# One Trainium2 kernel, diagonal softmax: y of five steps loaded through ScalarE's queue, and all row sums of six steps on VectorE

## The chip, the cores and the metric

The kernel runs on one core of one Trainium2 chip. The metric is the device time of one execution in microseconds; the median of the timed runs counts. The core has a VectorE (DVE in the profile), a ScalarE (ACT), a SyncE (SP) that mainly issues transfers, and 16 DMA engines that move data between HBM and the on-chip memory of 128 partitions. SyncE and ScalarE each have a DMA queue of their own, q1 and q10 in the profile.

## The reference

For each of 8 batches, x and y are 4096 x 512 in float32. Of the product x yT only the diagonal is needed, that is, one dot product of 512 elements per row; a softmax over the 4096 dot products of a batch follows.

```python
def reference(x, y):
    gram = np.matmul(x, y.transpose(0, 2, 1))
    diag = np.diagonal(gram, axis1=1, axis2=2)
    diag = diag - diag.max(axis=-1, keepdims=True)
    exp = np.exp(diag)
    return (exp / exp.sum(axis=-1, keepdims=True)).astype(np.float32)
```

x and y together are 134.2 MB, each byte of which is read once. The output is 0.13 MB.

## The kernel before

Four batches (Q) lie side by side on the 128 partitions, 32 partitions each; a partition holds 128 rows of its batch (C). So the work is two halves of four batches. Each half is cut into four steps of R = 32 rows a partition, which makes S = 8 steps, numbered 0 to 7. A step loads 128 x 32 x 512 elements of x and as many of y, 8.39 MB each.

The on-chip memory has two places for x, `xs[0]` and `xs[1]`, used in turn, and only one for y, `ys`. A small buffer `side` holds K = 6 rows of y.

Steps 0 to 5 are one loop, lines 123 to 134. In step t:

- `load_x` (line 65) and `load_y` (line 68) are issued by SyncE. x(t) may be issued when the sums of step t-2 have freed its place; y(t) when the first 26 rows of products of step t-1 have been made and the other 6 rows of y copied away.
- ScalarE copies the last 6 rows of y into `side` (line 126).
- VectorE multiplies the first 26 rows of x by `ys`, in place (line 72), then the last 6 rows by `side`.
- VectorE sums 30 rows of products (line 75), and ScalarE the last W = 2 rows (line 80).

At the end of step 3 the softmax of the first half begins (`exps`, line 101), and in step 4 it is ended (`normalize`, line 109). Step 6 splits its work otherwise: part of y is copied into a free part of x's other place (line 140), and ScalarE sums 30 of the 32 rows. Step 7 loads x and y in nine pieces, all on SyncE, and makes each row's dot product with one VectorE instruction (line 85). The softmax of the second half and the output follow.

The order of instructions on each engine is the order in which the kernel writes them, and an instruction that waits holds up all that stands behind it on its engine. On SyncE the loads thus stand as x(0), y(0), x(1), y(1), x(2) and so on. In this text x(t) and y(t) are the loads of step t, and "the sums" or "the products" of a step are its instructions of lines 75 and 72.

Of the kernel before, what the change touches and what calls it, by code (L numbers as in the profile page):

```python
# [1 line left out]

# [5 lines left out]


@with_exitstack
def kernel(
    ctx: ExitStack,
    tc: tile.TileContext,
    x: bass.AP,
    y: bass.AP,
    out: bass.AP,
):
    nc = tc.nc
    ctx.enter_context(tc.manual_schedule())  # L20
    f32 = mybir.dt.float32
    Alu = mybir.AluOpType
    Act = mybir.ActivationFunctionType
    X = mybir.AxisListType.X
    B, N, D = x.shape
    P = nc.NUM_PARTITIONS
    G = 32
    Q = P // G
    C = N // G
    R = 32  # L30
    H = R // 2
    K = 6
    W = 2
    F = H + 1
    L = 9
    S = B // Q * (C // R)


    xv = x.rearrange("(s b) (j c) d -> s (b j) c d", b=Q, j=G)
    yv = y.rearrange("(s b) (j c) d -> s (b j) c d", b=Q, j=G)  # L40
    ov = out.rearrange("(s b) (j c) -> s (b j) c", b=Q, j=G)

    big = ctx.enter_context(tc.tile_pool(name="big", bufs=1))
    small = ctx.enter_context(tc.tile_pool(name="small", bufs=1))


    xs = [big.tile([P, R, D], f32, name=f"xs{i}") for i in range(2)]
    ys = big.tile([P, R, D], f32, name="ys")
    side = big.tile([P, K, D], f32, name="side")

    diag = [small.tile([P, C + 2 * i], f32, name=f"diag{i}") for i in range(B // Q)]
    res = [small.tile([P, C], f32, name=f"res{i}") for i in range(B // Q)]

    def columns(t, r0, n):
        c0 = t % (C // R) * R + r0
        return slice(c0, c0 + n)

    def rows(t, r0, n):
        return xs[t % 2][:, r0 : r0 + n, :]

    def dots_of(t, r0, n):
        return diag[t * R // C][:, columns(t, r0, n)]

    def load_x(t, r0, n):
        nc.sync.dma_start(out=rows(t, r0, n), in_=xv[t * R // C, :, columns(t, r0, n), :])  # L65

    def load_y(t, r0, n):
        nc.sync.dma_start(out=ys[:, r0 : r0 + n, :], in_=yv[t * R // C, :, columns(t, r0, n), :])  # L68

    def products(t, r0, n, yt):  # L70
        xt = rows(t, r0, n)
        nc.vector.tensor_tensor(out=xt, in0=xt, in1=yt, op=Alu.mult)  # L72

    def sums(t, r0, n):
        nc.vector.tensor_reduce(out=dots_of(t, r0, n), in_=rows(t, r0, n), axis=X, op=Alu.add)  # L75

    def sums_act(t, r0, n):
        for r in range(r0, r0 + n):
            row = xs[t % 2][:, r, :]
            nc.scalar.activation(out=row, in_=row, func=Act.Copy, accum_out=dots_of(t, r, 1))  # L80

    def dots(t, r0, n):
        for r in range(r0, r0 + n):
            xt = xs[t % 2][:, r, :]
            nc.vector.scalar_tensor_tensor(  # L85
                out=xt, in0=xt, scalar=1.0, in1=ys[:, r, :], op0=Alu.mult, op1=Alu.mult,
                accum_out=dots_of(t, r, 1),
            )

    def over_quadrant(name, column, op, negate=False):  # L90

        got = small.tile([P, 1], f32, name=name)
        nc.vector.tensor_reduce(  # L93
            out=got, in_=column.to_broadcast([P, G]), axis=X, op=op, negate=negate, apply_transpose=True
        )
        return got

    def largest(out, d):
        nc.vector.tensor_reduce(out=out, in_=d, axis=X, op=Alu.max)  # L99

    def exps(i, d):
        mxp = small.tile([P, 1], f32, name=f"mxp{i}")
        largest(mxp, d)
        nmx = over_quadrant(f"nmx{i}", mxp, Alu.max, negate=True)
        sump = small.tile([P, 1], f32, name=f"sump{i}")
        nc.scalar.activation(out=res[i], in_=diag[i][:, :C], func=Act.Exp, bias=nmx, scale=1.0, accum_out=sump)  # L106
        return sump

    def normalize(i, sump):
        total = over_quadrant(f"sum{i}", sump, Alu.add)  # L110
        rc = small.tile([P, 1], f32, name=f"rc{i}")
        nc.vector.reciprocal(out=rc, in_=total)  # L112
        nc.vector.tensor_single_scalar(out=res[i], in_=res[i], scalar=rc, op=Alu.mult)  # L113

    nc.vector.addr_align(128, offset=0, max_nops=0)
    nc.scalar.addr_align(128, offset=0, max_nops=0)

    nc.sync.drain()  # L120
    nc.sync.drain()  # L121

    for t in range(S - 2):
        load_x(t, 0, R)
        load_y(t, 0, R)
        nc.scalar.activation(out=side, in_=ys[:, R - K :, :], func=Act.Copy)  # L126
        if t == C // R:
            normalize(0, sump)
        products(t, 0, R - K, ys[:, : R - K, :])
        products(t, R - K, K, side)  # L130
        sums(t, 0, R - W)
        sums_act(t, R - W, W)
        if t == C // R - 1:
            sump = exps(0, diag[0])

    t = S - 2
    load_x(t, 0, R)
    load_y(t, 0, R)
    spare = rows(t + 1, R - L, L)
    nc.scalar.activation(out=spare, in_=ys[:, F - L : F, :], func=Act.Copy)  # L140
    products(t, 0, F - L, ys[:, : F - L, :])
    products(t, F - L, L, spare)
    products(t, F, R - F, ys[:, F:, :])
    sums(t, R - W, W)
    sums_act(t, 0, R - W)
    largest(diag[1][:, C + 1 :], diag[1][:, : C - 2 * R])


    t += 1
    upto = {load_x: 0, load_y: 0}  # L150
    done = 0
    for load, n in (
        (load_x, H - 1), (load_y, F), (load_x, 8), (load_y, 10), (load_x, 6), (load_y, 3), (load_x, 2), (load_y, 2), (load_x, 1)
    ):
        load(t, upto[load], n)
        upto[load] += n
        both = min(upto.values())
        dots(t, done, both - done)
        done = both
        if done == F:  # L160
            largest(diag[1][:, C : C + 1], diag[1][:, C - 2 * R : C - R + H])

    met = small.tile([P, C - R], f32, name="met")
    nc.scalar.activation(out=met, in_=diag[1][:, : C - R], func=Act.Copy)  # L164

    for p in range(0, P, H):
        nc.sync.dma_start(out=ov[0, p : p + H, :], in_=res[0][p : p + H, :])
    normalize(1, exps(1, diag[1][:, C - R + H :]))
    nc.scalar.dma_start(out=ov[1], in_=res[1])


# [1 line left out]
_INS = ['x', 'y']  # L173
_OUTS = [((8, 4096), 'float32')]


# [23 lines left out]
```

## Time and profile before

| what | value |
|---|---|
| time, median of 3 runs | 320.38 us (320.29 to 320.44) |
| span of the profiled execution, first to last instruction | 318.8 us |
| around the span, median less span | 1.6 us |
| VectorE busy | 241.7 us (76%) |
| ScalarE busy | 49.8 us (16%) |
| 26 products of a step on VectorE | 14.03 us |
| 6 products | 3.35 us |
| 30 sums | 16.15 us |
| one row sum on ScalarE | 0.617 + 0.187 us |
| copy of 6 rows of y on ScalarE | 2.76 us |
| read from HBM | 134.22 MB, 421 GB/s over the span |

The profiled execution has no separate time beside its span; the 1.6 us are taken from the timed runs. In the views, L72 is line 72 of the kernel; `xs<-in_x_dram` is a transfer into `xs`; "SPq" and "ACTq" are the issues of transfers by SyncE and ScalarE; the time in brackets or after "waited for" is idle time of the engine that waits. The view of a window cuts it into 40 equal slices and gives what DMA moved in each, in GB/s; a packet is booked at its start, so a slice can show more than DMA can move.

### The profile page before, as it was taken

The numbers are of one execution on the slowest core, as the hardware profiler recorded it, in microseconds if no ns is written. First come the engines' busy times: TensorE is split into PE (matmuls) and PEld (weight loads), VectorE is DVE, ScalarE is ACT, GpSimd is POOL, SyncE is SP. The second block draws the span as 40 slices with busy tenths as digits, with TensorE's granted clock in tenths as the row PEclk, the third lists the DMA queues.
The fourth block names the chain that finished last, engine by engine and source line by source line (L and its number), as shares of the span: only waits on it lengthen the run. The fifth ranks groups of instructions, "written<-read, shape, count | busy, mean of one in ns | idle before, by whom it ended". The sixth has DMA issues, their size and how long they took to land.

```text
span 318.8 us, 315 instructions
## 1 busy us (share of the span) xinstructions
DVE 241.7 (76%) x98; ACT 49.8 (16%) x97; POOL 0.2 (0%) x4
## 2 busy tenths in 40 slices
DVE  0000069995899939999399994999939998599996
ACT  1000030100301003010120103000030100596700
POOL 0000000000000000000000000000000000000000
DMA  9999999999999999999999999999999999999993
GB/s 372 419 395 469 452 395 452 469 395 395 493 428 395 469 452 395 428 477 411 395 485 436 395 469 452 395 403 493 419 395 469 452 395 452 394 440 410 429 411 112
DMA packets 3714, 134.37 MB, mean 421 GB/s; under 512 B 512, under 2 KB 768, under 8 KB 1280
## 3 DMA queue, kind: packets, MB, share of 16 engines
q1 hardware_dynamic: 3568, 134.29, 97.7%
q10 hardware_dynamic: 144, 0.07, 0.1%
q14 instruction: 2, 0.02, 0.0%
HBM read 134.22 MB, written 0.13 MB: 421 GB/s over the span
## 4 chain that ended last, share of the span: by engine, by line
DMA 65%; DVE 33%; SPq 1%; issue 0%; ACT 0%; DVEq 0%
DMA ys<-in_y_dram 65%; DVE xs L72 32%; DVE xs L85 0%; SPq L65 0%; SPq L68 0%; DVE res L113 0%; DVE sum L93 0%; DVE nmx L93 0%; ACT res L106 0%; DVE mxp L99 0%; DVE rc L112 0%; DVEq L72 0%; SPq L121 0%; SPq L120 0%
## 5 line engine op out<-in xcount | busy, mean ns | idle before, releaser
L72 DVE TENSOR_TENSOR xs<-xs,ys 128x13312 f32<-128x13312 f32 (+2 forms) x8 | 96.7, 12091 | 71.9 <-DMA ys<-in_y_dram 71.9
L75 DVE TENSOR_REDUCE diag<-xs 128x30 f32<-128x15360 f32 (+1 forms) x7 | 98.1, 14020 | 0.2
L80 ACT ACTIVATE xs<-xs 128x512 f32<-128x512 f32 x42 | 25.9, 617 | 90.4 <-DVE xs L72 90.4
L126 ACT ACTIVATE side<-ys 128x3072 f32<-128x3072 f32 x6 | 16.6, 2763 | 124.1 <-DMA ys<-in_y_dram 124.1
L85 DVE SCALAR_TENSOR_TENSOR xs<-xs,ys 128x512 f32<-128x512 f32 x32 | 19.9, 687 | 1.1 <-DMA ys<-in_y_dram 1.0
L72 DVE TENSOR_TENSOR xs<-xs,side 128x3072 f32<-128x3072 f32 x6 | 20.1, 3351 | 0.0
L80 ACT ACTIVATION_READ_ACCUMULATOR xs<-xs 128x1 f32 x42 | 7.9, 187 | 0.0
L140 ACT ACTIVATE xs<-ys 128x4608 f32<-128x4608 f32 x1 | 4.0, 4043 | 20.0 <-DMA ys<-in_y_dram 20.0
L106 ACT ACTIVATE res<-diag,nmx 128x128 f32<-128x128 f32 x2 | 0.8, 402 | 30.1 <-DVE nmx L93 30.1
L72 DVE TENSOR_TENSOR xs<-xs,xs 128x4608 f32<-128x4608 f32 x1 | 5.0, 4951 | 0.0
L85 DVE DVE_READ_ACCUMULATOR xs<-xs,ys 128x1 f32 x32 | 2.6, 82 | 0.0
L126 ACT ACT_TABLE_LOAD x1 | 1.3, 1283 | 1.2 <-PEq L184 1.2
L93 DVE TRANSPOSE_TENSOR_REDUCE sum<-sump 128x1 f32<-128x32 f32 x2 | 0.4, 212 | 1.2 <-ACT res L106 1.2
L113 DVE TENSOR_SCALAR res<-res,rc 128x128 f32<-128x128 f32 x2 | 0.6, 286 | 0.1
L99 DVE TENSOR_REDUCE mxp<-diag 128x1 f32<-128x128 f32 (+1 forms) x2 | 0.5, 229 | 0.1
L93 DVE TRANSPOSE_TENSOR_REDUCE nmx<-mxp 128x1 f32<-128x32 f32 x2 | 0.4, 211 | 0.1
L99 DVE TENSOR_REDUCE diag<-diag 128x1 f32<-128x64 f32 (+1 forms) x2 | 0.4, 202 | 0.0
L112 DVE RECIPROCAL rc<-sum 128x1 f32<-128x1 f32 x2 | 0.3, 164 | 0.1
L106 ACT ACTIVATION_READ_ACCUMULATOR res<-diag,nmx 128x1 f32 x2 | 0.4, 186 | 0.0
L164 ACT ACTIVATE met<-diag 128x96 f32<-128x96 f32 x1 | 0.3, 283 | 0.0
L184 POOL MEMSET const-bfloat16-1.0<- 128x1 bf16 x1 | 0.1, 102 | 0.0
L184 POOL MEMSET const-uint8-127<- 128x1 uint8 x1 | 0.1, 101 | 0.0
(2 smaller groups left out, 0.2 us busy)
## 6 DMA issues: line engine op xcount, KB each, us to landing
ys<-in_y_dram SPq DMA_DIRECT2D x1, 4352.0 KB, 14.9
xs<-in_x_dram SPq DMA_DIRECT2D x1, 3840.0 KB, 14.2
ys<-in_y_dram SPq DMA_DIRECT2D x1, 2560.0 KB, 12.9
xs<-in_x_dram SPq DMA_DIRECT2D x1, 2048.0 KB, 19.4
xs<-in_x_dram SPq DMA_DIRECT2D x1, 1536.0 KB, 16.3
ys<-in_y_dram SPq DMA_DIRECT2D x1, 768.0 KB, 17.7
xs<-in_x_dram SPq DMA_DIRECT2D x1, 512.0 KB, 18.5
ys<-in_y_dram SPq DMA_DIRECT2D x1, 512.0 KB, 19.3
```

The source lines that it names most:

```text
L72: nc.vector.tensor_tensor(out=xt, in0=xt, in1=yt, op=Alu.mult)
L75: nc.vector.tensor_reduce(out=dots_of(t, r0, n), in_=rows(t, r0, n), axis=X, op=Alu.add)
L80: nc.scalar.activation(out=row, in_=row, func=Act.Copy, accum_out=dots_of(t, r, 1))
L85: nc.vector.scalar_tensor_tensor(out=xt, in0=xt, scalar=1.0, in1=ys[:, r, :], op0=Alu.mult, op1=Alu.mult, accum_out=dots_of(t, r, 1),)
L93: nc.vector.tensor_reduce(out=got, in_=column.to_broadcast([P, G]), axis=X, op=op, negate=negate, apply_transpose=True)
L99: nc.vector.tensor_reduce(out=out, in_=d, axis=X, op=Alu.max)
L106: nc.scalar.activation(out=res[i], in_=diag[i][:, :C], func=Act.Exp, bias=nmx, scale=1.0, accum_out=sump)
L112: nc.vector.reciprocal(out=rc, in_=total)
L113: nc.vector.tensor_single_scalar(out=res[i], in_=res[i], scalar=rc, op=Alu.mult)
L126: nc.scalar.activation(out=side, in_=ys[:, R - K :, :], func=Act.Copy)
L140: nc.scalar.activation(out=spare, in_=ys[:, F - L : F, :], func=Act.Copy)
L164: nc.scalar.activation(out=met, in_=diag[1][:, : C - R], func=Act.Copy)
```

## The change

The y loads of steps 1 to 5 are no longer written at the head of their step for SyncE's queue. Each is written one step earlier, behind the 26 products that free its place, and is issued by ScalarE. x stays on SyncE's queue, as do y of step 0 and all loads of steps 6 and 7. The last two row sums of steps 0 to 5 move from ScalarE to VectorE, which then sums all 32 rows with one instruction.

```diff
-    def load_y(t, r0, n):
-        nc.sync.dma_start(out=ys[:, r0 : r0 + n, :], in_=yv[t * R // C, :, columns(t, r0, n), :])
+    def load_y(t, r0, n, queue=nc.sync):
+        queue.dma_start(out=ys[:, r0 : r0 + n, :], in_=yv[t * R // C, :, columns(t, r0, n), :])
...
     for t in range(S - 2):
         load_x(t, 0, R)
-        load_y(t, 0, R)
+        if t == 0:
+            load_y(t, 0, R)
         nc.scalar.activation(out=side, in_=ys[:, R - K :, :], func=Act.Copy)
         if t == C // R:
             normalize(0, sump)
         products(t, 0, R - K, ys[:, : R - K, :])
+        if t < S - 3:
+            load_y(t + 1, 0, R, nc.scalar)
         products(t, R - K, K, side)
-        sums(t, 0, R - W)
-        sums_act(t, R - W, W)
+        sums(t, 0, R)
         if t == C // R - 1:
             sump = exps(0, diag[0])
```

## The prediction

> **What bounds the kernel now.** I read the page's first lines, then the chain of waits, then one step of the timeline, then the DMA view of a few short windows. The page says that VectorE is busy for 76% of the span, yet the queue that carries the loads is full:
>
> ```profile
> span 318.8 us, 315 instructions
> DVE 241.7 (76%) x98; ACT 49.8 (16%) x97; POOL 0.2 (0%) x4
> q1 hardware_dynamic: 3568, 134.29, 97.7%
> HBM read 134.22 MB, written 0.13 MB: 421 GB/s over the span
> ```
>
> Queue q1 (SyncE's) keeps the 16 DMA engines at work for 97.7% of the span. The chain in order of time shows how that looks inside the steps:
>
> ```profile
> 56.62 24.50 DMA ys<-in_y_dram
> ...
> 81.21 14.04 DVE xs L72
> ...
> 95.30 24.52 DMA ys<-in_y_dram
> ...
> 119.91 14.04 DVE xs L72
> ```
>
> The chain alternates "26 products, y load" and repeats every 38.70 us (81.21 to 119.91). It names VectorE for 14 us of each step, but that is not 14 us in which DMA rests. The stretches say so (columns: stretch, length, DVE busy, ACT busy, POOL busy, PE clock, DMA share, GB/s):
>
> ```profile
> 42.51:81.21 38.70, 33.44 (x3) 4.03 (x6) 0.00 (x0) 1.00 1.00 434
> 81.21:119.91 38.70, 33.45 (x3) 4.10 (x6) 0.00 (x0) 1.00 1.00 434
> 119.91:158.61 38.70, 33.45 (x4) 4.11 (x6) 0.00 (x0) 1.00 1.00 434
> 158.61:197.31 38.70, 34.60 (x8) 4.65 (x8) 0.00 (x0) 1.00 1.00 434
> ```
>
> DMA share is 1.00 in every step. A step moves x and y, 2 x 128 x 32 x 512 x 4 B = 16.78 MB; at 434 GB/s that is 38.7 us, the whole period. So the kernel is a stream of loads without a hole. The first step's products start at 42.51; the last piece of the other seven pairs of loads releases VectorE at 313.26, 270.75 us for 7 x 38.7 = 270.9. There is no idle DMA time to win back. The head (about 3 us above two loads) and the tail (318.8 - 313.3 = 5.5 us) are not touched.
>
> **How much cover each load has.** A load is 8.39 MB, 19.35 us. On each of 16 engines it is 8 packets (a 9.7 us window in mid-load has 64 packets for 4.19 MB, so 64 KB each), 2.42 us a packet. A y load takes 24.50 us from issue to landing, so it queues behind x. The smallest load-independent delay is seen at the end: the last output is issued by ScalarE at 316.43, and a window there shows its first packet at 317.30, so 0.87 us. Around 78 us the packets of all engines run in waves (slices of 0.1 us, starting at 76.0):
>
> ```profile
> GB/s 0 0 0 0 0 0 0 0 0 0 0 0 0 1966 1311 1966 655 0 1311 655 655 655 1311 0 0 0 0 0 0 0 0 0 0 0 0 0 0 1311 1966 1966
> ```
>
> A packet is booked where it starts, 655 is one packet. The wave of 77.3 to 78.3 (3, 2, 3, 1, 0, 2, 1, 1, 1, 2: 16 packets) is the last of y(1): it ends 79.7 on the first engine, 80.7 on the last, and VectorE starts at 81.21, about 0.5 us later. From an empty queue a load would thus take 0.87 + 19.35 + 0.5 + some 0.1 = 20.8 us. Spare of a y load: 24.5 - 20.8 = 3.7 us. Spare of an x load: x(2) is issued at 76.06, can start at 76.93, and is needed at 79.7 to 80.7: 2.8 to 3.8 us.
>
> **The change, part by part.**
>
> *y goes to ScalarE's queue.* Before, SyncE waits for exactly the same event, the 26 products:
>
> ```profile
> SPq L68 <- DVE xs L72: 169.3, 8, 53.6
> SPq L65 <- DVE diag L75: 114.4, 6, 19.1
> ```
>
> The x load ahead of it on SyncE is long issued (76.06 against 95.30), so y(2) leaves at 95.30, 0.05 us after the products end at 95.25. On ScalarE it leaves at the same time; an issue lasts 0.38 us there (the output's row) against 0.33 us, and the 0.05 us is under the 3.7 us spare. "As soon as its place is free" already held. Queued behind the waiting issue on ScalarE are the next copy into `side`, which needs that y anyway, and in step 3 the exponential, which runs at 192.82 while its y issue stands at 172.70. Nobody waits. On SyncE, x(t+2) no longer passes the y wait, but its own wait (for the sums) ends 19.4 us later, so it gains nothing. y(0), y(6) and y(7) stay on SyncE.
>
> *ScalarE's two row sums go, VectorE sums 32 rows.* Removed from ScalarE: 2 x (0.617 + 0.187) = 1.6 us a step, in time in which it then idles 20 us. Added to VectorE: 2/30 of 16.15 us = 1.08 us in each of six steps. VectorE idles 5.22 us before each y (3.24 us before step 4, where the softmax of the first half stands), so 4.1 and 2.2 us remain: nothing on the path. But x(t+2) waits for these sums, so it is issued 1.08 us later: x(2) at 77.14, at the engines at 78.01. Its spare falls to 1.7 to 2.7 us. Still no hole. If that cover were gone, each step would pay up to 1.08 us, 6.5 us in all.
>
> *Two queues at once.* This is the only real novelty, and the trace of before shows no load on another queue than q1, so it is bounded from both sides. y(2) reaches the engines at 96.17 and meets the last 2.9 to 3.9 us of x(2); x(3) meets the last packet of y(2). As long as an engine always has a packet, the order does not change when both are through, and the period stays 38.7 us. The Trainium skill speaks against a gain here: in "DMA: Bandwidth & Descriptors", "Issuing engines are not separate DMA queues", it says that loads issued by different engines run on the same 16 DMA engines and interleave. By that rule the sum stays at 0; the 434 GB/s with a share of 1.00 agrees.
>
> Lower end of this cost: an engine's 16 packets of 2.42 us fill the period of 38.70 us to within 0.1 us, the reading's own fineness; 0.1 us in each of seven steps would be -0.7 us. Upper end: the two rivals below, +4.4 and +6 us. I take 0, being nearest to the rows of four steps that stay at 1.00 whatever else happens in them.
>
> Sum: 0 (y issue) + 0 (ScalarE) + 0 (VectorE, hidden) + 0 (queues) + 0.1 (issue times). The profiled execution would keep its 318.8 us of span; the timed runs have 1.6 us around that (320.38). I say 320.5.
>
> **Rivals.**
>
> *A load's end waits its turn: slower.* A load is reported by a small marker packet behind its eight (the window 76 to 80 counts 8 packets under 512 B in the wave of load ends). If an engine takes turns between queues after each packet, an x packet goes ahead of y's marker. x(2) reaches the engines at 78.01; by the wave above, 12 engines are then in y(1)'s last packet and lose one turn (2.42 us), but 4 start it later and lose two (4.84 us); the slowest counts. One turn fits into the spares (3.7 and 2.7 us) and costs nothing. Two turns do not: y(2), issued 4.84 us late, leaves a hole of 4.84 - 3.7 = 1.1 us, and x(3) one of 4.84 - 1.1 - 2.7 = 1.0 us, 2.1 to 2.2 us for a pair of steps. Three pairs bound it at 6.6 us, one at 2.2; two pairs give +4.4: 324.8 us. It decides at 0.25 us: were x there after 78.3, all would be single turns. Against it: an engine that chooses its next packet only slightly ahead has that 0.25 us. The Trainium skill ("DMA: Bandwidth & Descriptors", "Queues, rings and completion order") says that an engine drains a whole packet of about 9 to 17 descriptors from one ring before it switches. Eight pieces and a marker are nine; were they one such packet, turns would fall between loads and this rival would be void; no run here shows which.
>
> *Changing queues costs time: slower.* From rest the first packets take longer: in windows of the first 8 us the waves start at 1.8 and at 4.7, 2.9 us apart instead of 2.42, so some 0.5 us. If every change of queue cost that, five changes a step over five steps are up to 12.5 us; half of it is +6: 326.4. Against: at the ends of loads within q1 the waves stay 2.42 us apart.
>
> *Two queues close small pauses: faster.* At most the 0.7 us above: 319.7. Against: the share is 1.00 already.
>
> **Chances.** No change 0.52 (own range 320.1 to 321.0), marker's turn 0.27, queue changes 0.13, faster 0.08. A measurement of this kernel can tell about 0.2%, 0.64 us, from no change. Both slower rivals are above it: slower 0.40, same 0.52, faster 0.08. The range reaches from 319.9, which leaves out most of the faster case, to 325.0, which takes in the middle of the marker case and leaves out its top and half of the queue changes: under 2 in 10 outside.
>
> **What would show it.** Right: y landings still 38.7 us apart, a DMA share of 1.00 in each stretch, y's issues on ScalarE at 56.6, 95.3 and so on, x's issues 1.08 us later (77.14, 115.83), VectorE idle about 4.1 us before each y, x landing later by a packet or two without effect. Marker's turn: products of step 1 start 2.4 or 4.8 us late while those of step 2 are nearly on time, every second step late, DMA share below 1.00 near 100 and 121 us. Queue changes: share at 1.00 but under 434 GB/s in steps 1 to 5. The forecast is wrong if products of step 6 start later than 275.4 (274.78 + 0.64).

## The result: 7.5 us slower, and the profile after

The changed kernel takes 327.86 us (median of four runs, 327.26 to 328.57) against 320.37 us: 1.0234 times as long, interval 1.0219 to 1.0248. The prediction said 320.5 us, with a range of 319.9 to 325.0. It was wrong; the time lies beyond the range, on the side of the two slower rivals. In the ratios of this text, runs more than 1.5% above the fastest of the same kernel are not counted.

The page's first parts of the changed kernel (columns as before):

```profile
span 326.3 us, 286 instructions
DVE 248.0 (76%) x98; ACT 41.8 (13%) x73; POOL 0.2 (0%) x4
q1 hardware_dynamic: 2848, 92.34, 66.6%
q10 hardware_dynamic: 864, 42.01, 30.2%
HBM read 134.22 MB, written 0.13 MB: 412 GB/s over the span
```

The five y loads, 42 MB, are now on q10. Both queues together hold the DMA engines for 96.8% of 326.3 us, 315.9 us; before it was 97.8% of 318.8 us, 311.8 us (q1 97.7%, q10 0.1%). The bytes are the same. So of the 7.5 us some 4.1 are packets that take longer, and only some 3.4 are time in which engines stand idle. VectorE has 6.3 us more work, close to the 6 x 1.08 that was worked out. The chain in order of time (start, length, what):

```profile
42.27 14.04 DVE xs L72
...
56.39 26.82 DMA ys<-in_y_dram
...
83.30 14.04 DVE xs L72
...
97.41 24.17 DMA ys<-in_y_dram
...
121.68 14.04 DVE xs L72
...
135.79 27.68 DMA ys<-in_y_dram
...
163.57 14.04 DVE xs L72
```

The y loads no longer all take 24.5 us: they take 26.8, 24.2, 27.7, then 22.6, 28.5 and, on SyncE again, 23.2. On a grid of 38.70 us from 42.27, the products of steps 1 to 6 start 2.3, 2.0, 5.2, 3.4, 7.4 and 6.0 us late. Every second step adds lateness, and the next one wins back only a part. Step 7 adds 1.8 us: from the start of step 6's products to that of the last four dot products it takes 40.3 us (280.49 to 320.79) instead of 38.5. The stretches between these starts (length, DVE, ACT, POOL, clock, DMA share, GB/s):

```profile
42.27:83.30 41.03, 34.51 (x3) 2.70 (x2) 0.00 (x0) 1.00 1.00 434
83.30:121.68 38.38, 34.52 (x4) 2.77 (x2) 0.00 (x0) 1.00 0.98 410
121.68:163.57 41.89, 34.51 (x4) 2.76 (x2) 0.00 (x0) 1.00 1.01 435
163.57:200.42 36.85, 35.68 (x9) 3.32 (x4) 0.00 (x0) 1.00 0.99 416
200.42:243.15 42.73, 34.51 (x3) 2.70 (x2) 0.00 (x0) 1.00 0.98 417
243.15:280.49 37.34, 34.52 (x4) 2.75 (x1) 0.00 (x0) 1.00 0.97 407
280.49:320.79 40.30, 37.40 (x67) 22.92 (x62) 0.00 (x0) 1.00 0.96 404
```

The first two long steps are not short of DMA: 434 and 435 GB/s, a share of 1.00. In them DMA moves more than the step needs, because part of the next x goes ahead of the end of y. The loss comes in the steps after, at 410 and 416 GB/s. From the third long step on, every step is below the rate of before, the long one too (417 GB/s). The rate falls further than the share: at 410 GB/s it is 6% down, and the share only 2%, so there too packets take longer.

How x gets ahead is seen at the end of y(1). Two windows of the changed kernel, 79.6 to 80.6 and 82.6 to 83.1 us (queue: packets, MB, share):

```profile
q1 hardware_dynamic: 16, 1.05, 242.9%
q10 hardware_dynamic: 11, 0.00, 0.6%
...
q1 hardware_dynamic: 6, 0.39, 181.5%
q10 hardware_dynamic: 5, 0.00, 0.6%
```

On q10 only markers are left, packets of 4 B that report a load's end. In the first window 11 of 16 engines send theirs. All 16 start their first packet of x(2). The other 5 engines do so ahead of their marker, and these five markers follow only when that packet is through, 2.42 us later. VectorE waits for the last of them. In the kernel before, the window of 79.6 to 80.8 us holds all 16 markers. At the end of y(3) two engines put a packet of x ahead of their marker, and the last of them was late already. At the end of y(5) all 16 do: the window of 238.8 to 240.4 us has 16 packets of q1 and no marker, that of 241.2 to 242.8 us the 16 markers. It is one packet each time.

And how the loss comes after it: y(2), issued at 97.41, in the window of 97.4 to 101.4 us (slices of 0.1 us):

```profile
GB/s 655 0 0 0 0 0 0 0 0 0 0 0 0 0 0 0 0 2622 655 0 1311 655 1311 655 0 655 0 655 655 0 0 0 0 655 655 0 0 0 0 0
q10 hardware_dynamic: 16, 1.05, 70.7%
```

The first value is x(2)'s last packet. x(2) ended from 99.1 on, and y(2)'s first packets start over 1.8 us, from 99.1 to 100.9, the last 3.5 us after the issue. Some engines had nothing to do meanwhile. And q10's share, 70.7% of 4.0 us for one packet on each of 16 engines, makes 2.83 us a packet, where 2.42 is usual. At the end of y(2), with hardly an engine idle, the first packets of x(3) are as long (window of 117.8 to 121.8 us, 2.82 us a packet):

```profile
q1 hardware_dynamic: 16, 1.05, 70.5%
```

### The profile page after: what moved, and what is told of

It is laid out like the page before. It is cut to its first block, busy times and chain, and to the rows that moved or that the text cites. A ratio compares the mean times of both kernels' runs of the same rounds, so it can differ in the third digit from the quotient of the medians.

```text
span 326.3 us, 286 instructions
## 1 busy us (share of the span) xinstructions
DVE 248.0 (76%) x98; ACT 41.8 (13%) x73; POOL 0.2 (0%) x4
## 4 chain that ended last, share of the span: by engine, by line
DMA 66%; DVE 32%; SPq 1%; issue 1%; ACT 0%; DVEq 0%; ACTq 0%
DMA ys<-in_y_dram 66%; DVE xs L72 31%; DVE xs L85 0%; SPq L65 0%; SPq L68 0%; DVE res L113 0%; DVE sum L93 0%; DVE nmx L93 0%; ACT res L106 0%; DVE mxp L99 0%; DVE rc L112 0%; DVEq L72 0%; ACTq L68 0%; SPq L121 0%; SPq L120 0%
## 5 line engine op out<-in xcount | busy, mean ns | idle before, releaser
L75 DVE TENSOR_REDUCE diag<-xs 128x32 f32<-128x16384 f32 (+1 forms) x7 | 104.5, 14934 | 0.2
L80 ACT ACTIVATE xs<-xs 128x512 f32<-128x512 f32 x30 | 18.4, 614 | 2.8 <-DVE xs L72 2.8
L80 ACT ACTIVATION_READ_ACCUMULATOR xs<-xs 128x1 f32 x30 | 5.6, 186 | 0.0
```

## The experiments

Theory M: the end of a y load waits its turn behind an x packet of the other queue, and the loads issued from that late point find engines that are already empty. Rival C: an engine loses time at each change of queue. Rival A: ScalarE's queue itself is slower.

**The sums alone.**

```diff
 # kernel before
-        sums(t, 0, R - W)
-        sums_act(t, R - W, W)
+        sums(t, 0, R)
```

> Only the sums move: VectorE sums all 32 rows in steps 0 to 5, every load stays on SyncE's queue. Theory M (with two queues the end of a y load waits its turn behind an x packet, and the loads that follow then come too late to find the engines busy): no effect, 320.4 us, at most +0.5, because x(t+2) is issued 1.08 us later but still lies behind y on the same queue. Theory C (each change of queue costs an engine a pause): 320.4. Theory A (ScalarE's queue itself is slower): 320.4. If the later x alone were the cause, it would show here as +1.08 us in each of six steps, 326.9.

Measured: 320.71 us against 320.61, ratio 1.0007, interval 0.9995 to 1.002. The y loads take 24.50, 24.74, 24.53, 24.51, 24.52 and 24.56 us. The 1.08 us of VectorE and the later x are hidden while one queue carries the stream.

**The queue alone.**

```diff
 # changed kernel
-        sums(t, 0, R)
+        sums(t, 0, R - W)
+        sums_act(t, R - W, W)
```

> Only the queue moves: y of steps 1 to 5 on ScalarE's queue, ScalarE keeps the two row sums, so x is issued 1.08 us earlier than in the changed kernel. M: more engines have x before the last y packet, so the first late y is 2.4 to 4.8 us late; in all +4 to +9 us, 324 to 329. C and A: as the changed kernel, 327.9.

Measured: 325.68 us (four runs from 324.3 to 329.2), ratio 1.0141, interval 1.0119 to 1.0164. By the ratio the second queue alone costs 4.5 us; the sums, free alone, cost some 3 us more beside it. C and A have no place for that difference. M may have one, as x is issued 1.08 us later after a late y, but no run shows that this is the reason. The first step goes as M said, with its products 2.4 us late; the pattern of every second step does not hold here, for step 2's are 4.3 us late.

**One queue, but ScalarE's.**

```diff
 # changed kernel
         if t == 0:
-            load_y(t, 0, R)
+            load_x(0, 0, R, nc.scalar)
+            load_y(0, 0, R, nc.scalar)
+            load_x(1, 0, R, nc.scalar)
...
         sums(t, 0, R)
+        if t < S - 3:
+            load_x(t + 2, 0, R, nc.scalar)
```

The other issues of x up to step 6 are taken out.

> All x and y loads of steps 0 to 5 and x of step 6 on ScalarE's queue, in the order of the kernel before; VectorE sums 32 rows; y of step 6 and step 7 on SyncE. One queue carries the stream, so no y end meets an x packet of another queue. M: the loss goes, 320.4 plus up to 0.6 for ScalarE's later start. C: goes too, 320.4 to 321. A: stays or grows, 328 or more, as twice the bytes run on that queue.

Measured: 323.09 us, ratio 1.0077, interval 1.0065 to 1.009: 2.5 us, more than the 0.6 allowed and far from A's 8. The timeline and the chain of this run show where:

```profile
1.16 2.55 ACTq L65 DMA_DIRECT2D xs<-in_x_dram  x1
...
44.72 14.04 DVE xs L72
...
83.41 14.04 DVE xs L72
```

ScalarE's first issue lasts 2.55 us, where SyncE's lasts 0.40 us, and y(0) is issued at 3.74 instead of 1.28. From there the steps are 38.7 to 39.1 us. So the head costs 2.45 us and the queue itself next to nothing. A falls.

**Smaller x packets.** Two runs with x in pieces of 8 rows, the second with step 6 too, and the same pieces on one queue as a control.

```diff
-        load_x(t, 0, R)
+        for r in range(0, R, R if t < 2 else R // 4):
+            load_x(t, r, R if t < 2 else R // 4)
...
 # second run and control also
-    load_x(t, 0, R)
+    for r in range(0, R, R // 4):
+        load_x(t, r, R // 4)
```

> The changed kernel with x of steps 2 to 5 loaded in four pieces of 8 rows, so that an x packet is 16 KB and takes 0.6 us instead of 2.4. M: the end of a y load waits 0.6 to 1.2 us instead of 2.4, the products of step 1 start about 82.0 instead of 83.3, and little of the loss is left: 320.5 to 323. C: as many changes of queue or more, 328 or more. A: 327.9.

Measured: 325.17 us, ratio 1.0129, interval 1.0089 to 1.0168: above M's 323, below C's 328, so it decides nothing alone. Its y(1) took 24.98 us, but its y(5), which meets x of step 6, left whole there, 28.53 us. Hence the next two.

> The changed kernel with x of steps 2 to 6 in four pieces (x of step 6 too, which the run with x in quarters left whole, and whose y before it came 5 us late). M: every y end waits 0.6 to 1.2 us only; step 6's products start near 276 instead of 280.5; 321 to 323.5. C or A: 325 or more, as with step 6 whole.

> Control: the kernel before, one queue, with x of steps 2 to 6 loaded in four pieces of 8 rows. M, C and A: 320.4, within 0.5; smaller packets alone cost nothing while one queue holds the order. If pieces themselves cost, 321 to 323.

Measured: 322.70 us for two queues, ratio 1.0078, interval 1.006 to 1.0096; 322.16 us for one queue, ratio 1.0059, interval 1.0044 to 1.0073. The control is not free, though 320.4 us was expected first: four pieces cost 1.8 us. But with small packets the second queue, and the sums with it, add only 0.5 us to that, instead of 7.5. That is within M's 321 to 323.5 and below the 325 of C and A. Step 6's products start at 276.24 us, where M had said 276. The chain with two queues, then with one:

```profile
56.37 25.10 DMA ys<-in_y_dram
...
81.56 14.04 DVE xs L72
...
134.03 25.67 DMA ys<-in_y_dram
```

```profile
56.43 24.49 DMA ys<-in_y_dram
...
81.02 14.03 DVE xs L72
...
133.99 24.80 DMA ys<-in_y_dram
```

y(1) is 0.6 us late and y(3) 0.9, where whole x packets made it 2.3 and 3.2. A turn of 16 KB takes 0.6 us, one of 64 KB 2.42. The delay follows the size of the other queue's packet.

**Smaller y packets.** y of steps 1 to 5 in four pieces on ScalarE's queue, x whole.

> The changed kernel with y of steps 1 to 5 in four pieces of 8 rows on ScalarE's queue, x whole on SyncE's: y's packets take 0.6 us and x's 2.4. M: each of the last two or three y packets and y's last marker waits behind an x packet, 3 to 4 turns of 2.4 us, so the products of step 1 start 5 to 10 us late (86 to 91 us), and each such step loses some 4 to 9 us: 333 to 347. C: one more change of queue for each small packet, at 0.5 us a change 2 us a step, 338 at most, with lateness spread over all steps. A: 327.9.

Measured: four runs from 325.1 to 339.8 us, median 333.5, too wide for a ratio. In the profiled one, the fastest, step 1's products start at 83.50, one turn late and not three or four. ScalarE's four issues of y(1) also take 6.0 us together, where one takes 0.38, so the run changes more than the size of packets. It decides nothing on C. It shows that M's number of turns was overdrawn, at least in that execution; the three longer ones have no profile.

**How late a load may be issued, on one queue.**

```diff
 # kernel before
-        sums(t, 0, R - W)
-        sums_act(t, R - W, W)
+        sums(t, 0, R)
+        sums(t, 0, 4)
```

> One queue (SyncE's), VectorE sums all 32 rows and then the first 4 rows once more (2.15 us of VectorE), so x(t+2) is issued 3.2 us later than in the kernel before and 2.15 us later than with the sums moved alone. It measures how much later a load may be issued before the engines run dry. The prediction's figure (0.87 us from issue to first packet, spare 1.7 to 2.7 us with the sums moved) says 0 to 0.5 us a step at most: 320.4 to 323. The traces of the loads that met idle engines in the changed kernel (1.0 us to the first, 2.6 us to the last engine, first packet 0.5 us longer) say that engines run dry by 0.5 to 1.5 us in each of the six x loads: 324 to 329.

Measured: ratio 1.0135, interval 1.0105 to 1.0165, some 4.3 us. (Its four runs spread from 323.6 to 330.4; the interval rests on the two lower ones, the profile is that of the highest and shows more loss than they have.) In that profile x(2) is issued at 79.09, and the window of 79.8 to 81.6 us shows

```profile
GB/s 0 0 0 0 0 2913 5826 1457 1456 2913 0 0 0 1456 0 0 0 0 0 0 0 0 0 1456 1456 0 0 0 0 2913 0 0 0 0 1456 0 0 0 0 0
...
q1 hardware_dynamic: 32, 1.05, 166.4%
```

in slices of 0.045 us, one packet 1456: the first engines start x(2) at 80.05, 0.95 us after the issue, the last at 81.35, 2.25 us after it. y(1)'s last markers are at 80.60. The 16 first packets take 166.4% of 1.8 us, some 2.99 us each. So 2.15 us of delay to x, nearly the size of one turn, empties the engines and makes packets longer without any second queue. The prediction's 0.87 us fits only the first engine.

**Which y loads cost.** First y(1) alone on ScalarE's queue, then y(1), y(3) and y(5). The edit of the second run is shown; the first has `(1,)` in place of `(1, 3, 5)`.

```diff
 # changed kernel
-        if t == 0:
+        if t not in (1, 3, 5):
             load_y(t, 0, R)
...
-        if t < S - 3:
+        if t + 1 in (1, 3, 5):
             load_y(t + 1, 0, R, nc.scalar)
```

> The changed kernel with y of step 1 alone on ScalarE's queue, y of steps 2 to 5 back on SyncE's; VectorE still sums 32 rows. It prices one late load end. M: the products of step 1 start 2.3 us late (83.3), y(2) and x(3) then start from near rest on SyncE's queue too, and 1.5 to 3 us stay: 322 to 323.5. C: one fifth of the 7.5 us, 1.5: 321.9, lost in steps 0 and 1 only in GB/s and not as a late marker. A: 321.9.

> The changed kernel with y of steps 1, 3 and 5 on ScalarE's queue (the three that came late in it) and y of steps 2 and 4 on SyncE's. M: steps 1, 3 and 5 late as before, the loads after them start from near rest whatever their queue, so most of the loss stays: 325.5 to 328.5. C and A: three fifths of 7.5 us, 4.5: 324.9 or less.

Measured: 325.01 us with y(1) alone, ratio 1.0131, interval 1.0098 to 1.0165; 329.05 us with three, ratio 1.0271, interval 1.0248 to 1.0295. Three loads on the second queue cost at least as much as five (the intervals touch at 1.0248), and more than M's 325.5 to 328.5. C, which counts changes of queue, allowed 4.5 us. It falls as the cause.

One load alone costs 4.2 us, more than M's 1.5 to 3. Its chain:

```profile
56.34 26.91 DMA ys<-in_y_dram
...
83.34 14.04 DVE xs L72
...
97.43 24.50 DMA ys<-in_y_dram
...
136.12 25.44 DMA ys<-in_y_dram
...
175.75 24.82 DMA ys<-in_y_dram
...
214.75 25.30 DMA ys<-in_y_dram
```

After the one late end everything is on one queue again, and yet later loads take up to 25.4 us. One thing seen is how far apart the engines run. The DMA view counts the ends of y(3) as packets under 512 B, first in the kernel before (window 157.1 to 158.1 us), then in this run (windows 158.4 to 159.4 and 158.4 to 161.4):

```profile
DMA packets 32, 1.05 MB, mean 1049 GB/s; under 512 B 16, under 2 KB 16, under 8 KB 16
q1 hardware_dynamic: 32, 1.05, 242.9%
```

```profile
DMA packets 26, 0.85 MB, mean 852 GB/s; under 512 B 13, under 2 KB 13, under 8 KB 13
...
DMA packets 44, 1.84 MB, mean 612 GB/s; under 512 B 16, under 2 KB 16, under 8 KB 16
```

Before, all 16 ends come within 1 us. Here 13 do, and the other three follow, the last 2.7 us after the first. The ends of each load from y(2) to y(5) lie 2.6 to 2.8 us apart in this run, 0.9 to 1.2 us before. An engine that once started late has as many packets to move as the others and stays late, and each load lands with the slowest. The other thing is that packets take longer: by the two queues' shares, 97.5% of 323.5 us, the engines are held for 315.4 us instead of 311.8, and that is most of the 4.7 us by which the span grew. What each of the two costs by itself no run separates.

## Why the prediction was wrong, point by point

- **y leaves no earlier: right.** The issues on ScalarE stand at 56.39 and 97.41, 0.08 and 0.07 us after the products before them end.
- **ScalarE's and VectorE's work is hidden: right** while one queue runs (1.0007 for the sums alone). Beside the second queue the same sums cost some 3 us (1.0234 against 1.0141), which the sum of the prediction had at 0. 32 sums took 17.22 us, 1.07 more than 30.
- **"Two queues at once ... I take 0": wrong, and the step that failed.** This term measured 4.5 us by itself and 7.5 us with the sums. The four steps at a share of 1.00 spoke of rate, and the rate did hold: the first step at two queues still shows 434 GB/s. What they could not show is the order in which packets leave. The load that is waited for ends behind a packet of the load that is not, 2.42 us late, and the loads issued from that late point come late for the engines: some wait, and the first packets take longer.
- **The marker's turn, at 0.27: the mechanism that happened.** Steps 1, 3 and 5 add lateness, as it said, and engines are short of work near 100 us. Two of its signs did not come: step 2 is not nearly on time but 2.0 us late, and near 121 us hardly an engine is idle, there packets are longer. The number of turns was wrong too. I had 12 engines with one turn and 4 with two in step 1; 11 had none, 5 had one. The two turns were what I let decide the case; one turn was enough.
- **The spare: mis-sized, and it decided the choice.** I took 0.87 us from the last output, a transfer of 64 KB, as the way from issue to engine, and got 3.7 us of spare for y and 1.7 to 2.7 for x. A whole load that meets idle engines starts 0.95 us after its issue on the first and 2.25 us on the last; in the changed kernel up to 3.5 us. The first packet is 0.5 us longer on top, as the waves at the kernel's start had shown (2.9 us instead of 2.42). The first load's own row was in the trace of before, and I used it for a rival only. With some 2 us less spare, one turn of 2.42 us does not fit, and the case for "costs nothing" is gone. The row and the window of 0 to 4 us of the kernel before (slices of 0.1 us; the 82 is q14's) show it: issued at 0.83 us, it starts on the engines from 1.8 to 3.3 us, 1.0 to 2.5 us after the issue, and the share of 72.2% of 4.0 us makes 2.89 us a packet.

```profile
0.83 0.40 SPq L65 DMA_DIRECT2D xs<-in_x_dram  x1
...
GB/s 0 0 0 0 0 0 0 0 0 0 0 0 0 0 0 0 0 82 2048 1311 655 1311 655 655 1311 655 655 655 0 0 0 0 0 655 0 0 0 0 0 0
...
q1 hardware_dynamic: 16, 1.05, 72.2%
```

- **The rival's price, 4.4 us: too small.** It counted holes, two turns each, for two pairs of steps. It left out that packets take longer when loads come late, and that engines, once apart, can stay apart: one late end alone cost 4.2 us. That the 1.8 us of the last step come from this too is my reading; no run shows it.
- **Changing queues: not the cause.** y(1)'s first packets on q10, with the engines busy, take the usual 2.42 us. Longer ones stand where a load comes late for the engines, on one queue too: 2.99 us in the run with x issued later, which changes no queue. One sign of this rival did come, a rate that falls more than the share; its 0.5 us a packet was real and had another occasion.
- **Two queues faster: no.** No stretch exceeds the rate of before by more than the reading.
- **The pages of the Trainium skill.** "DMA: Bandwidth & Descriptors", "Issuing engines are not separate DMA queues": loads from different issuers interleave on the same engines. The trace agrees, 16 packets of q1 among the markers of q10. The section "Queues, rings and completion order" of that page of the Trainium skill has an engine drain a packet of typically 9 to 17 descriptors before it switches. Here the measurement decides otherwise: five of 16 engines switched after y(1)'s eighth packet, ahead of its marker, and went back after one packet of x.

What stays open: the delay from issue to the last engine varies from 2.25 to 3.5 us in these traces, and I have no row that says what sets it. Longer packets are about half of the loss, and no run says what makes them longer when a load comes late. Nor does one say which engines put x ahead of their marker (5, 2 and 16 of them at the ends of y(1), y(3) and y(5)). Nor is it known why the kernels that empty the engines spread by several us from run to run, the one with y in pieces most of all.

## What to carry to other kernels

A stream at full DMA rate can still lose time to a second queue: what counts is which load's end is awaited, and whether another queue's packet can go in front of it. Keep loads that must land in order on one queue, or make the packets of the other small. And take the delay from issue to landing from a transfer of the same size on all engines, by its last engine, not from a small one's first packet.

## What the runs showed of the hardware that was not expected

- An engine may change queue between a load's last data packet and its 4-byte marker: 2.42 us for a 64 KB packet in between, 0.6 us for one of 16 KB.
- A load of 8.39 MB that meets idle engines starts on them over 1.3 us or more (0.95 to 2.25 us after the issue), and its first packets of 64 KB take 2.9 to 3.0 us on the mean, where 2.42 is usual.
- After a single late load end the engines' ends stayed 2.6 to 2.8 us apart from y(2) to y(5), on one queue; with the longer packets that end cost 4.2 us in all.
- ScalarE's first transfer issue took 2.55 us, where SyncE's took 0.40 us.
